# Attention output projection: the sample tokens' side stream entered at tile 7 of the first chunk

## Chip, cores and metric

The program runs on one core of one Trainium2 chip. The metric is the device time of one execution in microseconds (us); times of the trace are counted from the start of its span. The engines are called as in the profile: PE (TensorE, matmul), PEld (its weight loads), DVE (VectorE), ACT (ScalarE), POOL (GpSimd) and SP (SyncE, which here only issues DMAs).

## What is computed

The reference is one inference step of a two-layer decoder. Layer 0 mixes tokens with a recurrent block (RG-LRU), layer 1 with sliding-window attention; each is followed by a squared-ReLU MLP. Two groups of tokens share all weights: 1024 prompt tokens, and 8 sample tokens that attend to a cache of their own. The part that the change touches is the attention of the sample tokens and the output projection behind it:

```
def swa_sample(x, k_cache, v_cache, w_qkv, q_g, k_g, sinks, w_out):
    q, k, v = qkv_heads(x, w_qkv, q_g, k_g)
    k_all = jnp.concatenate([k_cache.astype(k.dtype), k], axis=1)
    v_all = jnp.concatenate([v_cache.astype(v.dtype), v], axis=1)
...
    o = sink_attention(q, k_all, v_all, dist, mask, sinks)
    y = o.reshape(n, s, Q_DIM) @ w_out
```

The prompt tokens go through the same projection `w_out`, so prompt and samples are put side by side: 1024 + 8 = 1032 columns.

## The kernel before

All values are held transposed, 128 features on the partitions and the 1032 tokens along the row; 1024 features are eight such tiles. The tokens are cut into three chunks of 344 columns (`cs(0)` to `cs(2)`); the eight sample tokens are the last columns of chunk 2. Every operand of a large matmul is split into a high and a low half, and a product is three matmuls: high by high, low by high, high by low (`passes`, L216). `split_act_dve` (L253) makes the halves: ACT casts the high one (L254), DVE subtracts it for the low one (L255).

The kernel is written with a library that orders each engine's instructions at build time by their place in the program and by when they are ready, and hands out buffers from pools. The pools that matter here: `S`, nine scratch tiles of 344 columns; `A`, the large tiles; and eight memory banks for matmul results, of which six go round in the order P, P, P, S, S, T (`ring`, L104), one is O and one, N, serves norm factors and the side stream.

**The output projection.** `out_proj` (L377) returns `entry_steps` (L340), a generator that yields after each input tile k, that is, after each three matmuls (`mm_steps`, L221). For the attention six of the eight input tiles (`early`) are multiplied ahead for output tiles m = 0 to 2 of chunks 0 and 1; that is run between the steps of the attention. The main loop then goes over the chunks c and in each over the output tiles m. A tile has eight steps, or two where the early part was done. Behind each tile DVE adds the residual into an S tile (L363), ACT starts the DMA that spills it (L364), squares it for the norm (L273) and writes the scaled copy for the MLP (L366). Four or five tiles into the next chunk, `factors` (L372) turns the sums of squares of the chunk before into its norm factors, through bank N (L263, L264, then `rstd_m2`, L288 to L295). These are first used in the MLP.

**The side stream.** `samples` (L951) is a second generator: the attention of the eight sample tokens. Its parts, with the calls that it takes until it has ended:

- call 1: the norm factors of the queries (L953 on ACT, L955 on PE, `rstd_m2`, L958 to L961 on DVE);
- calls 2 to 17: sixteen matmuls with the cached keys (L967; each shows as two instructions in the profile);
- call 18: the softmax with two transposes (L970 to L984), and then seven calls that do nothing (`range(8)`, L985);
- calls 26 to 41: sixteen matmuls with the cached values (L990);
- call 42: the copy out of the bank (L993) and sixteen small copies that put the result where the projection reads it (L999).

The projection calls it once per step (`for s in side: next(s, None)`, L1093 to L1095). `between(m, c)` (L1030) runs ahead of each tile: it loads residuals and weights, at tile 6 of chunk 0 it issues the loads of the cache on SP's queue (`load_cache`, L931), at tile 1 of chunk 1 it appends the side stream, and at tile 0 of chunk 2 it splits the stream's result into the halves that chunk 2 multiplies:

```
            if (m, c) == (0, 2):
                for t in range(8):
                    split_act_dve(ohl[t][0], ohl[t][1], osm[:, t, :], slice(SEQ, T))
```

So by the order of the program chunk 2 stands behind the end of the side stream. In chunk 2, `after(m)` prepares the operands of the MLP's first matmuls (L396, L397); the MLP's matmuls are L530.

Of the kernel before, what the change touches and what calls it, by code (L numbers as in the profile page):

```python
# [60 lines left out]
def trunk(ctx: ExitStack, tc: tile.TileContext, I, O):  # L61
# [115 lines left out]
    for o in [("x", m) for m in range(4)] + LRU:  # L177
        if o[0] == "g":
            units.append(("gate", o[1], I["w_gate"][o[1]], W))
        elif o[0] in "xo":  # L180
            m = o[1] + (8 if o[0] == "x" else 0)
# [71 lines left out]
    def split_act_dve(hi, lo, src, sl, eng=dve):  # L253
        act.copy(r_(hi[:, sl]), src)  # L254
        eng.tensor_tensor(r_(lo[:, sl]), src, hi[:, sl], ALU.subtract)  # L255
# [437 lines left out]
    def attention(hs):  # L693
# [193 lines left out]
        def stage_b(j, between):  # L887
            t, b = STEPS[j]
            se, pt = ses[j % 4], B("PT"[j % 2] if j < J0 else "T")
            first = 1 if b == 0 else 0  # L890
            blocks = [(u, h) for u in range(2) for h in range(first, 2)]
            for x, (u, h) in enumerate(blocks):
                pe.transpose(pt[:, h * 256 + u * P:h * 256 + u * P + P], se[:, u, h * P:h * P + P], ident)  # L893
                for y in between[x::len(blocks)]:
                    next(y, None)
            if j % 2 == 0:
                live["pt", j // 2] = W("pt")
            src = pt[:, 256 * first:512].rearrange("p (x q) -> p x q", q=P)
            dst = live["pt", j // 2][:, 512 * first:D].rearrange("p (x t q) -> p x t q", t=2, q=P)[:, :, t % 2, :]
            (act.copy if t % 2 else dve.tensor_copy)(dst, src)  # L900
# [30 lines left out]
        def load_cache():  # L931
            z = S("z")
            sp.dma_start(z[:, 129:257], I["dist_s"])
            zs.append(z)
            for p in range(2):
                kt = A("kc")
                kv = kt[:, :D].rearrange("p (n j) -> p n j", n=NS)
                sp.dma_start(kv[:, :, 0:127], I["k_cache"][p])
                dve.tensor_copy(kv[:, :, 127], ks[:, p, :])
                sp.dma_start(O["ks"][p], kt[:, :D])  # L940
                kc.append(kv)
            for h in range(2):
                vt = A("vc")
                vv = vt[:, :D].rearrange("p (n j) -> p n j", n=4)
                for part in (slice(0, 112), slice(112, 127)):
                    sp.dma_start(vv[part], I["v_cache"][part, 4 * h:4 * h + 4, :])
                sp.dma_start(vt[127:128, :D], vnew[h:h + 1, :])
                sp.dma_start(O["vs"][h], vt[:, :D])
                vc.append(vv)
# [80 lines left out]
        def between(m, c):  # L1030
            if c < 0 or (m, c) == (3, 0):
                need(m + 1)
            if m >= 4 and c == 0:
                need(min(m + 2, M8))
            if (m, c) == (6, 0):
                load_cache()
            if (m, c) == (1, 1):
                side.append(samples())
            if (m, c) == (0, 2):
                for t in range(8):  # L1040
                    split_act_dve(ohl[t][0], ohl[t][1], osm[:, t, :], slice(SEQ, T))
# [17 lines left out]
        for j in range(NJ):  # L1059
# [20 lines left out]
            if j == J0 + 2:  # L1080
                srcs = [ohl[t] for t in range(8)]
                r1 = A("rt")
                rs["r1"] = r1
                xs, need, fill = out_proj("wo1", srcs, spill, "g_mlp1", r1, spill1, before=between, after=ahead(1),
                                          early=(4, 5, 0, 1, 2, 3))
                for t in range(4):
                    load_o(t, cs(1))
# [338 lines left out]
```

## Time and profile before

| what | value |
|---|---|
| time, median of three runs | 2005.2 us (2004.97 to 2010.05) |
| the profiled execution's own time | 2010.09 us |
| its span in the profile | 2008.3 us |
| mean granted clock of PE | 0.998 |
| PE busy, first page | 1991.1 us, 99% |
| DVE, ACT, POOL busy | 1394.2, 1021.7, 364.5 us |
| main loop of the projection | about 1262 to 1350 us |
| side stream in it | 1288.6 (L953) to 1318.0 us (end of L999) |

A profile is of one execution, so a sum of its durations is held against that execution's 2010.09 us, not against the median. A line of the profile names the engine, the source line, the operation, and out<-in by the names of the tiles; `x24` is a count. What stands in brackets behind a row is the idle time of the engine ahead of it and what ended it. The granted clock is the share of full speed that PE was given.

### The profile page before, as it was taken

What the parts mean: (1) busy time and instruction counts of PE and PEld (TensorE: products, weight loads), DVE (VectorE), ACT (ScalarE), POOL (GpSimd) and SP (SyncE); (2) the same over time, 40 slices, a digit from 0 to 9 for tenths busy, and PEclk for the clock granted to TensorE, in tenths of its full rate; (3) what the DMA queues carried; (4) which work ended last, traced back from release to release, by engine and by line L of the source; (5) the groups of instructions that cost most, each with busy time, mean ns of one, the idle gap of its engine ahead of it and who ended that gap; (6) DMA issues with size and microseconds to landing.
All of it is one profiled execution on the core that took longest, in us unless ns stands there. A gap on an engine that the chain in (4) does not pass through costs nothing.

```text
span 2008.3 us, 38944 instructions
## 1 busy us (share of the span) xinstructions
PE 1991.1 (99%) x15188; PEld 1956.3 (97%) x15188; DVE 1394.2 (69%) x2649; ACT 1021.7 (51%) x2021; POOL 364.5 (18%) x664
## 2 busy tenths in 40 slices
PE   9999999999999999999999999999999999999999
PEld 8999999999999999999999897999999999999999
DVE  8996638877675876666846767578767667666672
ACT  6576536544334655545546656455433436554550
POOL 2320000000001233221006658000000003323220
PEclk9999999999999999999999999999999999999999
DMA  5111232343435788877343545523443447888783
GB/s 179 53 43 53 82 141 78 127 164 134 157 128 209 223 212 219 236 210 164 121 112 94 136 114 165 194 72 109 149 159 127 162 147 251 215 216 222 194 195 106
DMA packets 117929, 305.04 MB, mean 152 GB/s; under 512 B 17512, under 2 KB 50032, under 8 KB 117744
## 3 DMA queue, kind: packets, MB, share of 16 engines
q1 hardware_dynamic: 61744, 135.55, 22.1%
q0 software_dynamic: 28352, 98.30, 19.2%
q10 hardware_dynamic: 27648, 68.70, 9.3%
q8 instruction: 119, 1.95, 0.4%
q14 instruction: 66, 0.54, 0.1%
HBM read 176.30 MB, written 113.51 MB: 144 GB/s over the span
## 4 chain that ended last, share of the span: by engine, by line
PE 92%; issue 2%; DVE 2%; DMA 1%; POOL 1%; ACT 1%; SPq 0%; DVEq 0%; POOLq 0%; ACTq 0%
PE bD L530 58%; PE bP L227 13%; PE bS L227 7%; PE bP L793 4%; PE bT L227 4%; PE bO L916 1%; PE bS L867 1%; PE bS L823 1%; PE bT L893 1%; PE bP L893 1%; DMA raw<-w_in 1%; POOL se L883 0%; DMA spill<-he 0%; DMA spill<-ho 0%; PE bN L757 0%
## 5 line engine op out<-in xcount | busy, mean ns | idle before, releaser
L530 PE MATMUL bD<-op,op 128*128 128x258 f32 x5376 | 648.2, 283 | 0.0
L530 PEld LDWEIGHTS bD<-op,op 128*128 128x128 f32 x5376 | 647.7, 190 | 0.2
L530 PE MATMUL bD<-tl,op 128*128 128x258 f32 x4704 | 568.3, 283 | 0.6 <-ACT ho L637 0.6
L530 PEld LDWEIGHTS bD<-tl,op 128*128 128x128 f32 x4704 | 567.0, 190 | 1.8 <-ACT ho L637 0.8
L543 POOL DMA_DIRECT2D tl<-hsum x196 | 115.3, 696 | 905.8 <-PE bD L530 428.5
L397 DVE TENSOR_TENSOR op<-ws,op 128x512 fp32r<-128x512 f32 (+2 forms) x288 | 170.4, 597 | 82.6 <-ACT op L396 82.6
L403 DVE TENSOR_TENSOR tl<-tl 128x516 fp32r<-128x516 f32 x196 | 130.7, 692 | 121.6 <-ACT tl L402 121.5
L637 ACT COPY ho<-bD 128x516 f32<-128x516 f32 x144 | 85.0, 590 | 246.7 <-PE bD L530 240.1
L396 ACT CAST op<-ws 128x512 fp32r<-128x512 f32 (+2 forms) x288 | 155.8, 550 | 56.0 <-DVE op L397 27.1
L397 DVE TENSOR_TENSOR op<-raw,op 128x512 fp32r<-128x512 f32 (+2 forms) x216 | 124.3, 595 | 57.6 <-ACT op L396 57.5
L637 ACT COPY he<-bD 128x516 f32<-128x516 f32 x144 | 83.9, 583 | 132.1 <-PE bD L530 123.8
L396 ACT CAST op<-raw 128x512 fp32r<-128x512 f32 (+2 forms) x216 | 114.5, 549 | 36.6 <-PE bD L530 22.6
L402 ACT CAST tl<-tl 128x516 fp32r<-128x516 f32 x196 | 114.9, 627 | 4.6 <-DMA tl<-hsum 4.6
L650 ACT ACTIVATE ho<-ho 128x1032 f32<-128x1032 f32 x32 | 34.2, 1069 | 107.4 <-DVE ho L649 107.4
L167 DVE TENSOR_TENSOR wl<-raw,wh 128x1024 fp32r<-128x1024 f32 (+1 forms) x57 | 66.1, 1165 | 26.0 <-ACT wh L166 16.8
L876 DVE CUSTOM_DVE_ANT_0 se<-bS,bias,nsink 128x256 f32<-128x256 f32 (+1 forms) x128 | 63.9, 521 | 22.1 <-PE bP L893 7.4
L879 ACT ACTIVATE se<-se,den 128x257 f32<-128x257 f32 (+1 forms) x128 | 62.9, 493 | 29.8 <-DVE den L876 21.7
L166 ACT CAST wh<-raw 128x1024 fp32r<-128x1024 f32 (+1 forms) x60 | 58.6, 986 | 37.7 <-DMA raw<-w_in 13.0
L870 POOL TENSOR_SCALAR bias<-con,aux 128x256 f32<-128x256 f32 (+1 forms) x128 | 64.2, 503 | 41.8 <-DVE den L876 17.2
L656 POOL DMA_DIRECT2D spill<-ho x32 | 28.5, 889 | 236.7 <-DVE ho L645 228.2
L793 PE MATMUL bP<-hh,wh 128*128 128x344 f32 x192 | 70.0, 364 | 0.0
L645 DVE TENSOR_TENSOR ho<-bD,ho 128x516 f32<-128x516 f32 x72 | 49.7, 690 | 22.9 <-PE bD L530 22.9
(320 smaller groups left out, 3771.3 us busy)
## 6 DMA issues: line engine op xcount, KB each, us to landing
tl<-hsum POOLq DMA_DIRECT2D x196, 258.0 KB, 7.9
raw<-w_up SPq DMA_DIRECT2D x64, 512.0 KB, 3.8
raw<-w_dn SPq DMA_DIRECT2D x64, 384.0 KB, 6.3
spill<-ho POOLq DMA_DIRECT2D x32, 516.0 KB, 6.8
spill<-he POOLq DMA_DIRECT2D x32, 516.0 KB, 8.6
hsum<-ho ACTq DMA_DIRECT2D x28, 516.0 KB, 3.6
hsum<-he ACTq DMA_DIRECT2D x28, 516.0 KB, 2.7
hsum<-ts ACTq DMA_DIRECT2D x28, 516.0 KB, 3.5
```

Source lines behind the costliest of these rows:

```text
L167: eng.tensor_tensor(r_(lo[:, sl]), raw[:, sl], hi[:, sl], ALU.subtract)
L227: pe.matmul(o, lhsT=r_(wt[:, col(k):col(k) + P]), rhs=r_(xt[:, cs(c)]), start=(k == first and a == 0), stop=(k == final and a == 2))
L396: act.copy(r_(t[:, 0:n]), src)
L397: dve.tensor_tensor(r_(t[:, n:2 * n]), src, t[:, 0:n], ALU.subtract)
L402: act.copy(r_(hi), lo)
L403: dve.tensor_tensor(r_(lo), lo, hi, ALU.subtract)
L530: pe.matmul(d[:, 512 * b:512 * b + QT], lhsT=r_(wt[:, j * P:j * P + P]), rhs=r_(xt[:, QT * b:QT * b + QT]), start=first and j == 0 and a = ...
L543: pool.dma_start(t[:, n:2 * n], src)
L637: last["copy"] = act.copy(t, f).ins
L793: pe.matmul(o, lhsT=r_(wt[:, k * P:k * P + P]), rhs=r_(xt[:, cs(c)]), start=(k == 0 and a == 0), stop=(k == M8 - 1 and a == 2))
L870: pool.tensor_scalar(bias2[:, o - n:o], distM[:, 256 - n:256], fac[:, t % 4, 1, b, u:u + 1], SLOPES[hd[u]], ALU.mult, ALU.mult)
L876: dve.tensor_tensor_reduce(se[:, u, 256 - n:256], s[:, u * 256:u * 256 + n], bias2[:, o - n:o], scale=fac[:, t % 4, 0, b, u:u + 1], scalar ...
```

## The change

One condition in `between`: the generator of the side stream is appended ahead of tile 7 of chunk 0 and no longer ahead of tile 1 of chunk 1.

```
-            if (m, c) == (1, 1):
+            if (m, c) == (7, 0):
                 side.append(samples())
```

The loads of the cache stay at tile 6 of chunk 0, the splitting of the result at tile 0 of chunk 2, and the calls one per step of the projection. Between the new place and the old one lie ten steps: eight of tile 7 and two of tile 0 of chunk 1.

## Prediction

> **What bounds the kernel now.** I read the page first, then the list of what TensorE (PE) waited for from 1240 to 1420 us, then the timelines of PE and of the vector engine (DVE) around the one wait that the list holds.
>
> ```profile
> span 2008.3 us, 38944 instructions
> ...
> PE 1991.1 (99%) x15188; PEld 1956.3 (97%) x15188; DVE 1394.2 (69%) x2649; ACT 1021.7 (51%) x2021; POOL 364.5 (18%) x664
> ```
>
> PE is busy for 99% of the span, so the change can win only what PE loses: idle time, or matmuls at a lower clock. In the stage that it touches, the list of waits has one row (total, times, longest, in us):
>
> ```profile
> PE bP L227 <- DVE ol L255: 1.7, 1, 1.7
> ```
>
> L227 is the projection's matmul and L255 the low half of the samples' columns: the third chunk cannot begin until the side stream has ended. The PE timeline shows it (start, duration, instruction, idle time before it):
>
> ```profile
> 1314.38 0.28 PE L990 MATMUL bN<-ssb,vc 128*128 128x8 f32 x2
> ...
> 1316.02 0.63 PE L227 MATMUL bP<-oh,wh 128*128 128x344 f32 x3
> 1316.49 0.48 PE L227 MATMUL bS<-oh,wh 128*128 128x344 f32 x2
> 1318.69 0.43 PE L227 MATMUL bP<-ol,wh 128*128 128x344 f32 x1 [1.72 <-DVE ol L255]
> ...
> 1319.75 0.41 PE L227 MATMUL bP<-ol,wh 128*128 128x344 f32 x1
> ...
> 1323.34 0.31 PE L227 MATMUL bP<-oh,wl 128*128 128x344 f32 x1
> ```
>
> The side stream's last matmul (L990) starts at 1314.38. Nine matmuls of tile 7 and five first matmuls of the third chunk, which need only high halves, follow; then PE stands until 1318.69. DVE spends that time on the stream's tail:
>
> ```profile
> 1314.70 0.29 DVE L993 COPY ssb<-bN 128x128 f32<-128x128 f32 x1 [1.65 <-PE bN L990]
> 1315.03 2.98 DVE L999 COPY aux<-ssb 64x8 f32<-64x8 f32 x16
> 1318.04 0.52 DVE L363 TENSOR_TENSOR y<-bT,x 128x344 f32<-128x344 f32 x1
> 1318.47 0.69 DVE L255 TENSOR_TENSOR ol<-aux,oh 128x8 fp32r<-128x8 f32 x8
> ```
>
> From the last L990 to the first ready low half are 4.3 us: one copy, sixteen small copies, the evacuation of tile 7, the first of eight subtractions. And the clock falls behind the stall (a window: its length, the busy time of PE, of its weight loads, of DVE, ACT and POOL, the granted clock, the DMA share):
>
> ```profile
> 1319.80:1323.20 3.40, 3.40 (x14) 3.40 (x13) 0.40 (x1) 0.13 (x1) 0.00 (x0) 0.50 0.03 12
> ```
>
> **The price of the stall.** At full clock a matmul takes 0.158 us, from this row of the chain of work (start, length, matmuls):
>
> ```profile
> 1270.67 11.38 PE bP L227 x72
> ```
>
> The row at 1316.49 holds two matmuls, so the next could start at 1316.49 + 2 x 0.158 = 1316.81; it starts at 1318.69: 1.88 us lost. From the start at 1319.75 to that at 1323.34 lie 13 steps: 3.59 us in place of 13 x 0.158 = 2.05, so 1.54 us are lost to the half clock. Together 3.42 us, 0.17% of the time.
>
> [...]
>
> **The change part by part.** No instruction is added or removed, no DMA is issued anew; the generator of the side stream is entered earlier. It gets one call per step of the projection (three matmuls). A full tile has eight steps; tiles 0 to 2 of the first two chunks have two, since six of their eight inputs were done ahead. The stream takes 42 calls: 1 for the query factors, 16 for L967, 8 for the softmax, of which all work is in the first, 16 for L990, and the last for L993 and L999. From tile 1 of chunk 1 to the end of that chunk there are 2 + 2 + 5 x 8 = 44, so L990 ends three steps before chunk 2, as the nine matmuls above show. From tile 7 of chunk 0 there are 8 + 2 + 44 = 54: ten steps more. L990 then ends after step 3 of tile 6, and 5 + 8 = 13 steps x 0.471 = 6.1 us of matmuls cover the tail in place of 1.4.
>
> Is the stream ready to go that early? Its inputs first:
>
> ```profile
> L948 SPq DMA_DIRECT2D o_vs<-vc x2: 338/352/367, 1278.3 to 1282.3; - x2
> ...
> L933 SPq DMA_DIRECT2D z<-dist_s x1: 400/400/400, 1275.5 to 1275.5; - x1
> ```
>
> The values are written out from 1282.3 at the latest, so they are in the memory by then; the distances leave at 1275.5. Tile 7 of chunk 0 starts later than most of that:
>
> ```profile
> 1281.88 0.33 PE L227 MATMUL bS<-oh,wh 128*128 128x344 f32 x1
> ```
>
> The distances are needed once L955 has been through ACT and DVE, the values not before L990, over 10 us later. The loads on SP's queue stay at their place in the program (tile 6 of chunk 0), and nothing that the stream issues goes to a DMA queue: no load is late by the move. Now the stream's own latency:
>
> ```profile
> L955 PE MATMUL bN<-ones,ssb x2: 166/208/250, 1289.6 to 1289.6; 128*128 128x1 f32 x2
> ...
> L967 PE MATMUL bN<-aux,kc x32: 170/256/277, 1291.0 to 1298.4; 128*128 128x8 f32 x32
> L990 PE MATMUL bN<-ssb,vc x32: 170/256/277, 1306.3 to 1314.4; 128*128 128x8 f32 x32
> L984 DVE COPY ssb<-bN x1: 290/290/290, 1301.8 to 1301.8; 128x128 f32<-128x128 f32 x1
> ```
>
> From L955 to the first L967 pass 1.4 us, from the last L967 to the end of L984 3.7 us. In the new place L967 ends by step 3 of tile 3 and L990 is called from step 4 of tile 4: nine steps, 4.2 us, just above the 3.7. So L990 is not late. Its 64 small matmuls cost the same PE time wherever they stand: zero.
>
> **What is late next.** One thing changes order. There is one bank N, and chunk 0's norm factors take it ahead of tile 5 of chunk 1. Today they fall into the gap of eight calls before L990; now L990 holds the bank at that place, so the factors come after L993, in tiles 6 and 7. Nobody needs them before the next stage, but their DVE work joins the tail:
>
> ```profile
> 1305.72 0.58 DVE L293 SCALAR_TENSOR_TENSOR q<-bN,vec,q 128x344 f32<-128x344 f32 x1 [0.36 <-ACT q L292]
> 1306.33 0.52 DVE L295 SCALAR_TENSOR_TENSOR rt<-q,r 128x344 f32<-128x344 f32 x1
> ```
>
> The worst order on DVE: 4.26 us of tail, less 0.43 for tile 7's evacuation, which is not ready yet, plus 1.10 for the factors, plus 2 x 0.52 for tile 6's evacuation and its sum of squares: 5.97 us against 6.1 of cover. At best the tail alone, 3.8 us, is inside it. If the subtractions are queued behind tile 7's evacuation, as today, PE waits for that: 0.52 + 0.17 = 0.7 us. Bounds of what stays: 0 and 0.7 us; I take 0.3, nearer to the small end, since the DVE order of today puts L255 right behind the copies once they are done.
>
> Does the next stage follow? DVE is nearly full there (windows):
>
> ```profile
> 1350.00:1370.00 20.00, 20.00 (x166) 19.90 (x165) 19.42 (x33) 14.96 (x29) 0.00 (x0) 1.00 0.20 63
> ```
>
> But DVE idles while PE stands and crawls, and waits for PE's results until then, so its queue moves forward with PE; the list of waits has no row there. I charge nothing; if DVE did not move, up to the whole 3.1 us would be given back (that is the price of "no change").
>
> **Sum.** 3.42 - 0.3 = 3.1 us. The profiled execution took 2010.09 us (span 2008.3 and 1.8 around it), so it would take 2007.0. The runs shown are 2004.97 to 2010.05 with a median of 2005.2, so the profiled one is at the upper end of a scatter that is wider than the gain. From the median: **2002.1 us**. A measurement of this kernel can tell about 0.3%, 6 us, from no change.
>
> **The rivals.** (1) *Only the idle time goes.* The granted clock may fall for its own reasons or not have fallen in the runs at 2005; then 1.88 - 0.3 = 1.6 us are won: 2003.6. For it: the trace has another half-clock stretch, behind 0.82 us of idle time in 3.6:
>
> ```profile
> 1203.50:1207.10 3.60, 2.78 (x27) 2.54 (x27) 3.23 (x12) 2.65 (x10) 1.53 (x6) 1.00 0.91 290
> 1207.10:1210.60 3.50, 3.50 (x16) 2.14 (x17) 2.64 (x13) 1.84 (x8) 2.70 (x6) 0.51 0.90 239
> ```
>
> Against it: the stretch at 1319.8 lies right behind the only wait of the stage. [...]
>
> (2) *The stream does not start earlier, or its wait moves on.* The instructions are ordered by readiness, not strictly by the text. If the scratch tiles (S, nine of them, handed out in the order of the program) keep the first step back, or DVE holds the gain in the next stage: 2005.2. For it: four S tiles of the stream already keep an evacuation waiting, that of tile 1 of chunk 1, whose last matmul starts at 1287.42 and which DVE takes at 1291.02:
>
> ```profile
> 1287.42 0.32 PE L227 MATMUL bT<-oh,wl 128*128 128x344 f32 x1
> ```
>
> ```profile
> 1290.94 0.16 DVE L295 SCALAR_TENSOR_TENSOR r<-q,r 128x1 f32<-128x1 f32 x1
> 1291.02 0.52 DVE L363 TENSOR_TENSOR y<-bT,x 128x344 f32<-128x344 f32 x1
> ```
>
> Against it: there are six banks in turn, 14 us of matmuls from tile 7 of chunk 0 to the tile that needs its bank again, so 3.4 us of delay do not reach PE; with that cover gone, they would cost 3.4 us.
>
> (3) *Slower: an evacuation that waits for its S tile stands ahead of the tail in DVE's queue.* In the new place the delayed factors hold S tiles from tile 5 to tile 7, and ssb and two sums of squares hold three more, so the evacuations of tiles 6 and 7 share what is left; each S tile comes free only when its spill has landed:
>
> ```profile
> L364 ACTq DMA_DIRECT2D spill<-y x48: 326/326/1449, 251.6 to 1350.9; - x48
> ...
> DMA to landing us min/median/max: 1.8/1.9/6.8
> ```
>
> DVE takes its queue in order, so copies and subtractions behind such an evacuation wait too. At the median landing PE would idle 1.9 + 0.52 + 0.17 = 2.6 us and lose 1.54 to the clock, 4.1 against 3.4 of today: 2005.9. At the longest it idles 7.5 us and loses the clock twice, 10.6: 7.2 more than today, 2012.4. It decides from a landing of 1.2 us on, if the order on DVE is that one. Against it: L363 shows no wait for a spill today.
>
> **How the numbers follow.** Forecast 0.52, rival (1) 0.13, (2) 0.10, (3) 0.25. Of the forecast's 0.52, 0.12 lie beyond -0.3%: the scatter of 5 us is as wide as that, and another half-clock stretch of 1.54 us may go as well. Of (3), 0.20 lie beyond +0.3%. So faster 0.12; within 0.40 + 0.13 + 0.10 + 0.05 = 0.68; slower 0.20. The range goes from 2004.97 - 3.42 - 1.54, and half a microsecond below, 1999.5, to the price of (3), 2012.5. The forecast's own range is 2000.0 to 2005.
>
> **What would show it.** Right: L990 ends in tile 6 of chunk 1; L263 for chunk 0 comes after it; no wait on L255 above 0.7 us; full clock at the start of chunk 2; the first L530 about 3 us earlier against the last matmul of chunk 0. Wrong: a wait on L255 or on a bank N with as long an idle time, a new half-clock stretch between 1282 and 1320, L363 waiting for a spill, or PE waiting for DVE's operands after 1350.

## The result and the profile after

The changed kernel takes 2003.41 us (median of 22 runs, 2002.57 to 2004.91) against 2005.53 us (22 runs, 2004.94 to 2010.05) of the kernel before: a ratio of 0.9987 with a 95% interval of [0.9981, 0.9993]. It is 2.1 us faster, 0.11%: within the 0.3% that the prediction called no change, inside its range, and 1.3 us above its 2002.1. The profiled execution of the changed kernel took 2002.95 us. Its page, by engine:

```profile
span 2001.2 us, 38937 instructions
...
PE 1987.5 (99%) x15188; PEld 1954.1 (98%) x15188; DVE 1394.0 (70%) x2649; ACT 1021.0 (51%) x2021; POOL 364.4 (18%) x664
```

Same instructions on each engine, 3.6 us less busy time on PE (PE is busy for longer with the same matmuls at half clock: 13 steps took 3.59 us in place of 2.05) and 7.1 us less span. The list of what PE waited for from 1240 to 1420 us, which had the one row on L255, is a header without rows:

```profile
engine line waited for: us in total, times, longest us
```

The PE timeline (start, duration, instruction) shows the end of the stream and the border of the third chunk:

```profile
1306.51 0.28 PE L990 MATMUL bN<-ssb,vc 128*128 128x8 f32 x2
...
1307.27 0.40 PE L263 MATMUL bN<-shi,ones 128*128 128x344 f32 x1
...
1313.17 0.32 PE L227 MATMUL bT<-oh,wl 128*128 128x344 f32 x1
1313.33 0.32 PE L227 MATMUL bP<-oh,wh 128*128 128x344 f32 x1
1313.48 0.32 PE L227 MATMUL bP<-ol,wh 128*128 128x344 f32 x1
```

The last L990 stands 6.8 us ahead of chunk 2's first matmul (1313.33 - 1306.51) where it was 1.6 (1316.02 - 1314.38). Chunk 0's norm factors (L263) now come behind it. Across the border the matmuls follow each other at 0.16 us. DVE in the same stretch:

```profile
1306.83 0.29 DVE L993 COPY ssb<-bN 128x128 f32<-128x128 f32 x1 [5.00 <-PE bN L990]
1307.15 2.97 DVE L999 COPY aux<-ssb 64x8 f32<-64x8 f32 x16
1310.16 0.17 DVE L255 TENSOR_TENSOR ol<-aux,oh 128x8 fp32r<-128x8 f32 x1
1310.24 0.51 DVE L363 TENSOR_TENSOR y<-bS,x 128x344 f32<-128x344 f32 x1
1310.67 0.47 DVE L255 TENSOR_TENSOR ol<-aux,oh 128x8 fp32r<-128x8 f32 x5
1311.05 0.57 DVE L293 SCALAR_TENSOR_TENSOR q<-bN,vec,q 128x344 f32<-128x344 f32 x1
...
1313.54 0.26 DVE L255 TENSOR_TENSOR ol<-aux,oh 128x8 fp32r<-128x8 f32 x2
```

The tail is the same copies and subtractions as before, 3.8 us from the last L990 to the end of the first low half, but now under tiles 6 and 7. Six of the eight low halves are done 2 us ahead of chunk 2. The last two start at 1313.54, after it has begun; they are first read in its seventh step, 6 x 0.47 = 2.8 us in, at 1316.1.

The windows over the border (length, busy PE, weight loads, DVE, ACT, POOL, granted clock, DMA share, GB/s) have PE full at full clock, where before had 1.68 us busy in 3.40 and then 3.40 us at a granted clock of 0.50. Before:

```profile
1316.40:1319.80 3.40, 1.68 (x11) 1.39 (x10) 3.19 (x20) 1.82 (x7) 0.00 (x0) 1.00 0.11 40
```

After:

```profile
1310.00:1313.40 3.40, 3.40 (x24) 3.40 (x23) 3.27 (x13) 1.93 (x6) 0.00 (x0) 1.00 0.29 102
1313.40:1316.80 3.40, 3.40 (x24) 3.40 (x23) 3.02 (x8) 3.25 (x9) 0.00 (x0) 1.00 0.15 53
```

Where the 7.1 us between the two profiled executions lie is read from the last group of the attention's matmuls (L916) and the first matmul of the MLP (L530) on the PE timeline. Before:

```profile
1262.90 1.08 PE L916 MATMUL bO<-pt,vt 128*64 128x256 f32 x8
1350.10 2.10 PE L530 MATMUL bD<-op,op 128*128 128x258 f32 x16
```

After:

```profile
1260.45 1.08 PE L916 MATMUL bO<-pt,vt 128*64 128x256 f32 x8
1343.90 8.36 PE L530 MATMUL bD<-op,op 128*128 128x258 f32 x68
```

The stage takes 83.45 us in place of 87.20: 3.75 less. Another 2.45 us were won ahead of it and 0.9 behind it, where the change touches nothing. The 2.45 have a half-clock stretch in them, at 1207 us (granted clock 0.51 over 3.50 us), which the kernel before had in its profiled execution and the changed one has not; the windows at that place after:

```profile
1203.50:1207.10 3.60, 2.78 (x26) 2.33 (x27) 2.91 (x13) 2.57 (x10) 1.84 (x6) 1.00 0.91 264
1207.10:1210.60 3.50, 2.86 (x22) 1.89 (x18) 3.22 (x17) 2.58 (x9) 3.29 (x8) 1.00 1.02 277
```

So half of the gap between the two profiles is scatter, and of the 3.75 us in the stage 1.54 are a half clock that not every execution of before need have. That is why the experiments below compare runs with a mean granted clock of 1.000 ("at full clock") beside the medians of all. At full clock the kernel before has medians of 2005.39, 2005.23 and 2005.55 us in the three sets of runs, and the changed kernel 2002.94 and 2003.05 us.

### The profile page after: what moved, and what is told of

Read it like the earlier page. It is cut to its first block, busy times and chain, and to the rows that moved or that the text cites. A ratio compares the mean times of both kernels' runs of the same rounds, so it can differ in the third digit from the quotient of the medians.

```text
span 2001.2 us, 38937 instructions
## 1 busy us (share of the span) xinstructions
PE 1987.5 (99%) x15188; PEld 1954.1 (98%) x15188; DVE 1394.0 (70%) x2649; ACT 1021.0 (51%) x2021; POOL 364.4 (18%) x664
## 3 DMA queue, kind: packets, MB, share of 16 engines
q8 instruction: 119, 1.95, 0.4%
## 4 chain that ended last, share of the span: by engine, by line
PE 96%; DVE 1%; POOL 1%; ACT 1%; issue 1%; DMA 0%; SPq 0%; DVEq 0%; POOLq 0%; ACTq 0%
PE bD L530 61%; PE bP L227 13%; PE bS L227 8%; PE bP L793 5%; PE bT L227 4%; PE bS L867 1%; PE bO L916 1%; PE bS L823 1%; PE bT L893 1%; PE bP L893 1%; DMA raw<-w_in 0%; POOL se L883 0%; PE bN L757 0%; DVE sq L278 0%; POOL bias L870 0%
## 5 line engine op out<-in xcount | busy, mean ns | idle before, releaser
L530 PE MATMUL bD<-op,op 128*128 128x258 f32 x5376 | 648.2, 283 | 0.0
L530 PEld LDWEIGHTS bD<-op,op 128*128 128x128 f32 x5376 | 647.7, 190 | 0.3
L530 PE MATMUL bD<-tl,op 128*128 128x258 f32 x4704 | 568.0, 283 | 0.0
L530 PEld LDWEIGHTS bD<-tl,op 128*128 128x128 f32 x4704 | 566.8, 190 | 1.0 <-ACT he L637 0.3
L397 DVE TENSOR_TENSOR op<-ws,op 128x512 fp32r<-128x512 f32 (+2 forms) x288 | 170.4, 597 | 81.2 <-ACT op L396 81.2
L397 DVE TENSOR_TENSOR op<-raw,op 128x512 fp32r<-128x512 f32 (+2 forms) x216 | 124.2, 595 | 57.7 <-ACT op L396 57.7
```

What stands on the lines that cost most here:

```text
L397: dve.tensor_tensor(r_(t[:, n:2 * n]), src, t[:, 0:n], ALU.subtract)
L530: pe.matmul(d[:, 512 * b:512 * b + QT], lhsT=r_(wt[:, j * P:j * P + P]), rhs=r_(xt[:, QT * b:QT * b + QT]), start=first and j == 0 and a = ...
```

## The experiments

The theory after the result: the gain comes from the **end** of the stream, which no longer stands between chunk 2 and its low halves. The rivals: the earlier **start** is what counts (other matmuls between the small ones, the norm factors in another place), or the gain is only a **clock** that happened not to fall.

**The end early, the start unchanged.** The kernel before, with one idle call in place of eight between the softmax and the values:

```
-            yield from range(8)
+            yield from range(1)
```

> The kernel before with the seven empty calls of the stream taken out: it starts at tile 1 of chunk 1 as before, but L990 ends ten of the projection's steps before chunk 2 (before: three). Theory 'end': only the end of the stream counts, PE no longer stands 1.88 us ahead of chunk 2, so 2003.5 us (ratio to before 0.9990) and no wait on L255. Rival 'start': the gain comes from the earlier start (key tiles and S tiles free sooner, evacuations at the seam sooner), so no change, 2005.5. Rival 'clock': each run of the kernel before also has 1.54 us of half clock behind the stall, so 2002.1.

Measured: 2003.55 us (11 runs, 2003.00 to 2008.41), 0.9986 [0.9977, 0.9994]. PE waits for nothing in the stage. At full clock 2003.49 (9 of 11 runs) against 2005.39: 1.90 us, the idle time of 1.88. All the idle time of the stall comes back with the start where it was. One of the 11 runs is at a clock of 0.997 all the same (2008.41).

**The start early, the end unchanged.** The changed kernel, with ten more idle calls:

```
-            yield from range(8)
+            yield from range(18)
```

> The changed kernel with 18 empty calls in place of 8: it starts at tile 7 of chunk 0 like the changed kernel, but its end stands where the kernel before has it, three steps before chunk 2. Theory 'end': the wait of 1.7 us on L255 is back, 2005.5 us, ratio to before 1.000. Rival 'start': the gain stays, 2003.4. Rival 'clock': as 'end'.

Measured: 2005.70 us (2005.02 to 2009.63), 0.9998 [0.9989, 1.0007]; at full clock 2005.28 (6 of 11) against 2005.39. The wait is back, as long as before, in the PE timeline:

```profile
1317.57 0.42 PE L227 MATMUL bP<-ol,wh 128*128 128x344 f32 x1 [1.72 <-DVE ol L255]
```

With the first run, this settles end against start. It has a second reading: the 3.40 us with the stall have the same 1.68 us of busy PE as before, and the clock does not fall behind them:

```profile
1315.50:1318.90 3.40, 1.68 (x11) 1.39 (x10) 3.22 (x19) 1.87 (x7) 0.00 (x0) 1.00 0.14 52
1318.90:1322.30 3.40, 3.40 (x24) 3.40 (x23) 0.99 (x3) 0.97 (x2) 0.00 (x0) 1.00 0.00 0
```

**A shorter tail, nothing moved.** The kernel before, with the sixteen small copies (L999) made into four of 64x32:

```
-            for t in range(8):
-                p, i = divmod(t, 4)
+            for p in range(2):
...
-                    dve.tensor_copy(osm[h, t, :], sv[h, :, p, u, i])
+                    dve.tensor_copy(osm[h, 4 * p:4 * p + 4, :], sv[h, :, p, u, :].rearrange("p n i -> p i n"))
```

> The kernel before with four copies of 64 x 32 in place of the sixteen of 64 x 8 (L999); start and end of the stream as before. The tail on DVE falls from 4.3 to about 2.3 us, and PE has 9 + 5 matmuls, 2.2 us, beside it. Theory 'end': the wait falls to 0 to 0.3 us, 2003.6 us (ratio 0.9990). Rival 'start': no change, 2005.5. Rival 'clock': 2002.1 to 2002.4.

Measured: 2004.80 us (2003.74 to 2005.80), 0.9989 [0.9980, 0.9998]; at full clock 2004.20 (6 of 11), 1.2 us less than before and 0.6 more than hoped for. PE still waits for L255:

```profile
PE bP L227 <- DVE ol L255: 0.4, 1, 0.4
```

DVE shows why. The copies took 0.79 us in place of 2.98, but then an operand of the MLP (L397) was taken ahead of the low halves:

```profile
1314.06 0.29 DVE L993 COPY ssb<-bN 128x128 f32<-128x128 f32 x1 [1.65 <-PE bN L990]
1314.38 0.79 DVE L998 COPY aux<-ssb 64x32 f32<-64x32 f32 x4
1315.21 0.70 DVE L397 TENSOR_TENSOR op<-x,op 128x516 fp32r<-128x516 f32 x1
1315.82 0.24 DVE L255 TENSOR_TENSOR ol<-aux,oh 128x8 fp32r<-128x8 f32 x2
```

The tail's length counts, as the theory has it; the expectation missed what DVE does with the time that comes free.

**The start one tile later**, at tile 2 of chunk 1, two steps behind the place of before:

```
-            if (m, c) == (1, 1):
+            if (m, c) == (2, 1):
```

> The kernel before with the stream begun at tile 2 of chunk 1, two steps later: L990 ends one step before chunk 2. Theory 'end': two steps of 0.47 us more of wait, 2.8 us of idle time in all, 2006.4 us without the clock, up to 2008 where the longer idle time brings the half clock in more runs. Rival 'start': two of twelve steps, under 0.4 us, 2005.9. Rival 'clock': 0.94 more and the same 1.54 as before, 2006.4 in each run.

Measured: 2009.30 us (2006.29 to 2013.33), 1.0011 [1.0002, 1.0020]. Only 2 of 11 runs are at full clock, 2006.29 and 2006.36, 0.9 us over before, as two steps of 0.47 make it; 7 have a clock of 0.998 or less. PE waits 0.4 us at the border of chunk 2 (for L254) and 1.9 us behind the five matmuls that follow (for L363, the evacuation of bank T, which DVE has ahead of the low halves). But the larger part is elsewhere: 10.20 us at half clock with PE fully busy, right behind sixteen key instructions in a row. Timeline and window:

```profile
1290.22 1.95 PE L967 MATMUL bN<-aux,kc 128*128 128x8 f32 x16
```

```profile
1293.10:1303.30 10.20, 10.20 (x42) 10.14 (x41) 2.00 (x7) 1.46 (x4) 0.00 (x0) 0.50 0.05 17
```

That was a new question: what brings the clock down where PE does not idle? The next runs take it up, beside the tail.

**The changed kernel again, and with the four copies.** The first is the kernel after as it is, the second has the edit of the third experiment on top.

> The changed kernel once more, beside the next three on one chip. Theory 'end': 1.88 us of idle time and 0.28 us of a short gap at L983 are gone and nothing of the wait stays, so runs at full clock lie 2.2 us under the full-clock runs of the kernel before (2003.1 against 2005.35), and the projection from its last L916 to the first L530 takes 82.75 us. If the half clock were the smaller part of it, the distance of the medians is larger than that of the full-clock runs.

> The changed kernel with four copies in place of sixteen (L999). Theory 'end': the tail is already hidden behind 13 steps of matmuls, so shortening it brings nothing: the same as the changed kernel within 0.3 us, full-clock runs at 2003. Rival: the DVE tail still costs something in the changed kernel (the last low halves come only at the start of chunk 2), then up to 0.5 us less.

Measured: 2003.57 us (0.9985 [0.9976, 0.9994]) and 2003.36 us (0.9986 [0.9977, 0.9994]); at full clock 2003.05 (7 of 11) and 2003.15 (8 of 11), against 2005.23 of before on the same chip. A tail that is 2.2 us shorter gives nothing once it is covered. The gain at full clock is 2.18 us, as expected, and the medians of all runs of this set lie 2.8 us apart (2006.41 and 2003.57). The projection takes 83.45 us from its last L916 to the first L530 (1260.81 to 1344.26), as in the first profile of the changed kernel, and not the 82.75 us expected.

**Small matmuls in a row.** The changed kernel, with both calls per matmul taken out of the stream, so that 32 key instructions and 32 value instructions each run back to back:

```
                     pe.matmul(...)     # L967, and the same at L990
-                    yield
```

> The changed kernel with the 32 key instructions (L967) in one call and the 32 value instructions (L990) in one call, so that each group runs back to back for 3.6 us in place of one pair per step; same work, no idle time, an earlier end. Theory 'idle' (the clock falls because PE stands still): full clock in the projection, 2002.9, as the changed kernel. Theory 'small matmuls' (matmuls of 8 columns back to back count as little work for the clock): half clock behind both groups in nearly every run, at least 1.7 us each, 2006 or more, granted clock 0.998 or less.

Measured: 2005.91 us (2004.01 to 2010.21), 1.0001 [0.9992, 1.0010]; none of 11 runs at full clock, 8 at 0.998 or less. In the profiled execution the 32 keys bring no half clock. Behind the values the clock falls, with no idle time in the 3.40 us ahead or in those at half clock:

```profile
1283.62 3.74 PE L967 MATMUL bN<-aux,kc 128*128 128x8 f32 x32
...
1290.81 3.63 PE L989 MATMUL bN<-ssb,vc 128*128 128x8 f32 x32
```

```profile
1292.30:1295.70 3.40, 3.40 (x29) 3.40 (x29) 1.09 (x6) 0.60 (x3) 0.00 (x0) 0.99 0.10 34
1295.70:1299.10 3.40, 3.40 (x14) 3.40 (x13) 3.14 (x20) 1.05 (x6) 0.00 (x0) 0.50 0.00 0
```

**The idle time filled.** The kernel before, with twelve matmuls of 344 columns that nobody reads ahead of chunk 2's splitting:

```
             if (m, c) == (0, 2):
+                fb = B("N")
+                for _ in range(12):
+                    pe.matmul(fb[:, :CH], lhsT=r_(ones), rhs=r_(ohl[0][0][:, cs(0)]), start=True, stop=True)
```

> The kernel before with 12 idle matmuls of 344 columns (result unused) put ahead of chunk 2, so that PE works through 1.9 us of the wait; the four first matmuls that ran ahead there now come later, 0.63 us. Full-clock runs at 2005.35 + 0.63 = 2006.0. Theory 'idle': the runs at a clock of 0.997 to 0.998, one in four of the kernel before, are gone. Theory 'small matmuls': they stay, one in four, since both bursts of the stream stay.

Measured: 2006.83 us (2005.77 to 2011.36), 1.0008 [0.9999, 1.0017]; at full clock 2005.88 (4 of 11). 3 of 11 runs stay at 0.997 or less, although PE now waits for L255 only 0.5 us. Together with the one low run of the first experiment, whose profile has no wait at all, this says that the low-clock runs of the kernel before are not all the stall's. Eleven runs are too few to tell shares apart: the third experiment, with 0.4 us of wait, had none at 0.998 or less.

**Two steps alone.** The start at tile 0 of chunk 1, two steps ahead of before and eight behind the change:

```
-            if (m, c) == (1, 1):
+            if (m, c) == (0, 1):
```

> The kernel before with the stream begun two steps earlier, at tile 0 of chunk 1: L990 ends five steps before chunk 2. Theory 'end': each step takes 0.47 us off the wait, so 1.88 - 0.94 = 0.9 us stay and full-clock runs lie at 2004.4 (kernel before 2005.3). Rival 'start': two of ten steps of the whole gain, 2004.9.

Measured: 2008.53 us (2004.60 to 2010.01), 1.0006 [0.9998, 1.0015]. Three runs at full clock (2004.60, 2004.92, 2005.15), and eight at 0.997. Their median is 0.6 us under before's 2005.55; the theory gives 0.94 and the rival 'start' 0.4, so these three runs do not tell the two apart. The chain of work (start, length, instructions) shows the norm factors of chunk 0 (L263, L264) on bank N just ahead of the values. The stream has gone two steps further by then, and sixteen value instructions run in a row where the kernel before has twelve. The windows show the price:

```profile
1302.54 0.15 PE bN L263
...
1305.53 1.93 PE bN L990 x16
```

```profile
1305.30:1308.70 3.40, 3.40 (x28) 3.20 (x27) 2.86 (x6) 2.10 (x4) 0.00 (x0) 1.00 0.16 55
1308.70:1318.90 10.20, 10.20 (x41) 10.20 (x40) 3.28 (x16) 2.47 (x8) 0.00 (x0) 0.50 0.05 17
```

A move of the same kind as the change, only shorter, gave no measurable gain: it took away part of the stall and made a longer burst. (In the profiled execution PE waits for L255 not at all, since it comes late to chunk 2 itself, at half clock.)

**One burst each.** The changed kernel, with the calls taken out at the keys alone, then at the values alone:

```
                     pe.matmul(...)     # L967 in one kernel, L990 in the other
-                    yield
```

> The changed kernel with the 32 key instructions (L967) in one call, the value ones (L990) one pair per step as before. Theory 'small matmuls': one back-to-back group of 3.6 us brings half clock in most runs, 2004.6 or more, and more where the pairs of L990 keep the clock down. If the pairs count as full work, one window of 3.4 us: 1.7 us over the changed kernel's 2003.0. Theory 'idle': 2003.0.

> The changed kernel with the 32 value instructions (L990) in one call, the keys as in the changed kernel. Behind the group stand only large matmuls. Theory 'small matmuls': one window at half clock in most runs, 2004.7. Theory 'idle': 2003.0.

Measured: 2007.88 us (1.0006 [0.9997, 1.0015]) and 2006.25 us (0.9998 [0.9989, 1.0007]); 9 of 11 runs each at 0.998 or less. The keys' burst takes 4.38 us, 0.9 more than the values' burst of as many instructions. Right behind it three matmuls of the projection take 1.06 us, as they do at a granted clock of 0.50 in two steps alone, and later 0.57 (chain of work):

```profile
1284.05 4.38 PE bN L967 x32
1288.43 1.06 PE bS L227 x3
...
1295.12 0.57 PE bP L227 x3
```

This kernel has a new wait as well (L263 for ACT, 1.5 us), so its time is not the clock's alone. The values' burst takes 3.48 us, and behind it the clock is at half for 3.40 us:

```profile
1298.50:1301.90 3.40, 3.40 (x31) 3.40 (x31) 0.51 (x3) 0.00 (x0) 0.00 (x0) 1.00 0.00 0
1301.90:1305.30 3.40, 3.40 (x14) 3.40 (x14) 3.06 (x23) 1.58 (x8) 0.00 (x0) 0.50 0.00 0
```

**No burst at all.** The changed kernel, with seven calls in place of one between the query factors and the keys, and five in place of eight between softmax and values, so that no two pairs stand side by side:

```
-            yield
+            yield from range(7)
...
-            yield from range(8)
+            yield from range(5)
```

> The changed kernel with six empty calls more ahead of the keys and three fewer behind the softmax: no two pairs of the stream stand back to back, against 12 instructions in a row in the changed kernel; L990 ends nine steps before chunk 2. Theory 'end': the wait stays hidden, full-clock runs at 2003.0 to 2003.3. Theory 'small matmuls': as many runs at full clock as the changed kernel or more; its runs at 0.999 that come from the attention ahead of it (a window at 1206 us) stay.

Measured: 2003.20 us (2002.67 to 2004.96), 0.9982 [0.9973, 0.9991]; at full clock 2002.99 (8 of 11), none at 0.998 or less. This is the changed kernel's time within the scatter: the burst of twelve keys that the changed kernel still has costs nothing that these runs can tell. None of the kernels tried is measurably better than the change.

## Why the prediction was right, and where it was off

- **The range says little.** It is 13 us wide, from the scatter of the runs below to the price of rival (3) above, and the change is worth 2. The forecast, rival (1) and rival (2) all lie within 0.3% of before, so that the time came out there does not tell them apart.
- **The bound and the stall: right.** PE is the bound, and the wait on L255 was the one loss in the stage that the change could reach. Its 1.88 us came back where the end alone was moved (1.90 at full clock), and not where the start alone was (0.1).
- **The count of steps: right.** L990 ends behind the fourth step (step 3) of tile 6, L263 comes after L993, and chunk 2 starts 6.8 us behind the last L990.
- **What stays of the wait: 0 in place of 0.3 us.** The order on DVE was near the best of the cases: the first low half is ready 3.8 us behind the last L990, and the evacuation at 1310.24 slipped in only behind it.
- **The half clock: the step that failed.** The sum took "1.54 us are lost to the half clock" from the profiled execution and subtracted it from the median of the runs. That term is in a part of the runs only: 19 of 98 runs of the kernel before have a granted clock of 0.998 or less, and none of 33 runs of the changed kernel. The stall's stretch, 3.40 us at a granted clock of 0.50, is 1.7 of 2005 us; by this estimate a run that has it alone shows as 0.999 and is not among the 19 (the profiled execution, with two such stretches, shows 0.998); but runs at 0.999 are about as frequent after, 13 of 33, as before, 35 of 98. The term lifts the mean (2006.27 against 2003.64 in the first 22 runs each, 2.6 us) more than the median (2.1), and how many of the 19 owe it to the stall stays open. The prediction itself had noted that the profiled execution stood at the upper end of the scatter. Without the term its sum is rival (1), 2003.6 against the 2003.41 measured. That this is so close is in part luck: rival (1) has a gain of 1.6 us and the runs 2.1, and it starts from a median of three runs, 2005.2, where 22 runs gave 2005.53.
- **A term that was not in the sum:** at full clock the gain is 2.18 us, 0.3 more than the idle time. Part of it is at the second transpose of the softmax (L983). Before, on the PE timeline, 0.43 us lie between its start and that of the matmul ahead, in place of 0.16:

```profile
1301.05 0.31 PE L227 MATMUL bS<-oh,wh 128*128 128x344 f32 x1
1301.48 0.30 PE L983 MATMUL bN<-con,e 128*128 128x128 f32 x1
```

After, one more matmul stands between the two transposes, and 0.29 us are left:

```profile
1294.02 0.32 PE L227 MATMUL bP<-ol,wh 128*128 128x344 f32 x1
1294.31 0.30 PE L983 MATMUL bN<-con,e 128*128 128x128 f32 x1
```

  That is 0.14 us, and it goes with the earlier start: the first experiment, with the start of before, still has 0.43 us there and gained 1.90. The other 0.16 were not located.
- **Rival (2), no change: refuted.** The stream started earlier, and the next stage followed: the first L530 moved with the border of chunk 2, and no wait on DVE's operands took the place of the one removed.
- **Rival (3), slower by an evacuation that waits for an S tile: not seen.** No row of L363 waits for a spill, and PE waits for nothing. That a wait of 7.5 us loses the clock twice, as its upper price had it, was an estimate; no run shows such a wait. What did turn such a move slower was something that neither the forecast nor a rival had: the clock under bursts, with the start two steps earlier (2008.53 us) or two later (2009.30).

## What to carry to other kernels

Of a side stream that feeds a later stage, look at where its last instruction and the tail behind it end, not at where it starts; what counts is the cover between that and the first reader, and once it is covered a shorter tail is worth nothing (2.2 us less of it: 2003.15 against 2003.05 us at full clock). When a stream of small matmuls is moved, see how many of them then run in a row (behind the wait for bank N sixteen caught up at once, in two steps alone), since a burst can cost more than the stall that it removes: behind those sixteen lay 10.20 us at a granted clock of 0.50, which is an estimated 5.1 us lost, against 1.88 of idle time in the stall. A loss that is seen in one profiled execution, above all one of the clock, is not taken off a median until the runs show how often it occurs.

## What the runs showed of the clock

The half clock here goes neither with idle time nor with the busy time of the profile. In the kernel before and in the second experiment the 3.40 us with the stall have the same 1.68 us of busy PE; behind them the granted clock was 0.50 in the one and 1.00 in the other. In the attention PE was busy for 2.78 of 3.60 us before and after, and the clock behind it was 0.51 before and 1.00 after. With the start one tile later PE stood for 2.3 of the 7.00 us around its two waits, and the clock was 1.00 in them and behind them:

```profile
1316.00:1323.00 7.00, 4.68 (x30) 4.11 (x30) 4.75 (x28) 3.08 (x11) 0.00 (x0) 1.00 0.06 22
1323.00:1330.00 7.00, 7.00 (x46) 7.00 (x46) 3.52 (x7) 2.13 (x5) 0.00 (x0) 1.00 0.08 28
```

On the other side, PE was busy for all of the 3.40 us ahead of the falls at 1308.7 (two steps alone) and 1301.9 (the values' burst). The windows show 3.40 us at a clock of 0.50 at 1319.8 in the kernel before, at 1295.7 with both bursts and at 1301.9 with the values' burst, and 10.20 us at 1293.1 with the start one tile later and at 1308.7 in two steps alone. At that clock 3.40 us held 14 matmuls (1319.8 before), at full clock 24 (1318.9 in the second experiment).

What the falls shown with a busy PE have ahead of them is a burst of small matmuls: sixteen keys in 1.95 us, sixteen values in 1.93, 32 values in 3.63 and in 3.48. That is 0.11 to 0.12 us for 8 columns, where a matmul of 344 columns takes 0.158; so in a burst PE multiplies few columns for the time that it is busy. Whether that is why the clock falls was not shown. A burst does not always bring it down: the 32 keys of the kernel with both bursts ran from 1283.62 to 1287.36, and the clock stayed at 1.00, while with the keys' burst alone it fell. The kernel with both:

```profile
1283.00:1286.50 3.50, 3.50 (x31) 3.36 (x29) 0.85 (x5) 0.28 (x2) 0.00 (x0) 1.00 0.06 22
1286.50:1290.00 3.50, 3.42 (x24) 3.08 (x24) 2.21 (x8) 1.08 (x4) 0.00 (x0) 1.00 0.05 17
```

What decides between the two stays open. That long bursts go with the low clock is borne out by the kernels that were made on purpose: the five with sixteen or more in a row have 7 to 9 of 11 runs at 0.998 or less, the three with fourteen and at most 0.5 us of wait on L255 together 4 of 33, and the changed kernel with twelve none of 33. Of the five, the start one tile later and the keys' burst have waits of 1.5 us and more as well, and two steps alone keeps a part of the stall; the other two have no wait above 0.3 us in the stage. Fourteen and twelve are the longest bursts of before and after, on the PE timelines:

```profile
1290.96 1.73 PE L967 MATMUL bN<-aux,kc 128*128 128x8 f32 x14
```

```profile
1283.31 1.50 PE L967 MATMUL bN<-aux,kc 128*128 128x8 f32 x12
```

So a part of the low-clock runs of the kernel before need not be the stall's, as the filled one showed.

The place in the attention lies in a stage that the change does not touch. The second experiment has the half clock there too, from 1206.5 on (0.50 in the two windows up to 1208.0); its profiled execution shows 0.999, as does that of the kernel with both bursts, which has the stretch at 1295.7. So runs at 0.999 may owe it to the attention; that was not shown for those without a profile.
